# A state-space layer's input projection in one full-fp32 product instead of three split ones, with its parameter work in wider operations

## The chip, the core and the metric

One core of a Trainium2 chip runs the whole program. The metric is the device time of one execution in microseconds (us), median over several runs; less is better. The engines are TensorE (PE; its weight loads are a row of their own, PEld), VectorE (DVE), ScalarE (ACT), GpSimd (POOL) and SyncE (SP), which here only starts DMA transfers. Each engine works through its own instructions strictly in the order in which the program gives them; engines wait for each other by semaphores.

## What is computed

Two layers of a decoder trunk on 256 positions with 2048 channels, batch 1. Layer 0 mixes tokens with a state-space (S5) layer, layer 1 with a gated recurrence; each is followed by a SwiGLU. Scale, shift and gate of every norm come from a conditioning vector through the big matrix `w_ada`. The change touches the S5 layer:

```python
h = rmsnorm(x, norm_g[i, 0]) * (1.0 + sc1) + sh1
u = h @ w_in                                   # the input projection: 2048 x 2048
ug = u.reshape(bsz, seq, 128, 16)              # 128 groups of 16 channels
dt = exp(log_dt); mag = exp(lr * dt)
a = mag * (cos(li * dt) + i sin(li * dt))      # 64 complex states per group
b = (a - 1) / lambda * B                       # (128, 64, 16)
s_l = a * s_(l-1) + b u_l                      # a scan along the 256 positions
y = real(C s) + d_skip * u
y = gelu(y); val, gate = split(y @ w_glu); out = val * sigmoid(gate)
```

## The kernel before

The activations lie channels by positions: `X` is 128 partitions x 16 tiles x 256 positions. A matrix product takes 128 output channels at a time (a tile), as a sum over 16 (or 11, or 22) blocks of 128 input channels.

**Products in three parts.** TensorE takes a rounded fp32 format (`F32R`) in one pass. To stay accurate, each operand is split in a high part and a rest: ACT copies the weights to `wh` (L453), DVE computes `wl = raw - wh` (L468), and `H` holds high and low part of the activations. In the S5 projection, `into` (L874 and on) issues for each block `wh*h0`, `wh*h1` and `wl*h0` (L877 to L879). Elsewhere the first two are one product 512 columns wide.

**The weight stream.** Class `Stream` holds one list of items of 1 MB or less, in the order in which they are used: weights (`w`), and rows of `w_ada`. The latter are either `a` (a multiply-and-sum on DVE, L472), or `p` and `q` (four products on PE side by side in four column strips, L480; every fourth item ends with an ACT eviction to `par`, L486, and later with `rows_out`, L495 to L501, which turns the row into columns). Loads go out on SP's queue into four buffers `raw` (`NRAW = 4`); `step` first asks for the load of the item four places ahead, which waits until that buffer is free. `used` and `ahead` split the next weights, and do the `a` and `p` items, whenever a half block of weights (a slot) has been used up.

**The S5 layer** (`s5_layer`) has a prologue and a loop of 16 rounds, one for each tile. The prologue runs the first 31 or so items, in which shift and scale of the first norm are computed, beside `prep` (tables of the powers of `a`, on DVE), the sums of squares (ACT squares, POOL adds them up, `sq_add`) and the first parameters. Then `norm` writes `H`.

In round `t` PE runs the 16 blocks of tile `t` of the projection, and between them, by the table `fill`, pieces of other tiles:
- `states(t-1)`: 8 products `pv` (L346) of the tile's input `U` with `G`, then a `chain` on DVE: turn the phases back, scan, turn forward (L356 to L367);
- `outs(t-2)`: 12 products into `py` (L385, L387), then 16 ACT gelus (L915), each on 32 partitions and 64 columns;
- `gen2(t+1)`: transposes of `gs` into `pg` (`tr`, L306), each half evicted by ACT into `G` (L307), and between them `tt`, products into `pt` (L314), which DVE completes (L316); in the next round ACT copies `pt` in 16 pieces into `T` (L320, called `late`). `pg` and `pt` have one buffer each.

After the blocks: `u2(t)`, 16 ACT copies of the tile into `U` (L329); `gen_p(t+1)`, the phase table of a tile, six DVE operations (L285 to L287) and an ACT copy into `d0` (L289); `gen_gl(t+2)`, which builds the tile's `gs` and `ls` from its B and C: 4 ACT copies (L258) and 16 POOL operations (L251, L267); `load_bc(t+3)`, a DMA on ACT's queue (L94).

Of the kernel before, what the change touches and what calls it, by code (L numbers as in the profile page):

```python
# [75 lines left out]
class S5:  # L76
# [3 lines left out]
    def __init__(self, nc, const, gen, ps, lam, bcd, ident):  # L80
        self.nc, self.const, self.gen, self.ps = nc, const, gen, ps
        self.lam, self.bcd, self.ident = lam, bcd, ident
        self.work = None
        self.gt = {}
        self.bct = {}

    def load(self):
        self.lam_t = self.const.tile([P, 4, 64], F32, name="s5lam")
        self.nc.sync.dma_start(self.lam_t, self.lam)

    def load_bc(self, t):
        if t < 16:
            bct = self.gen.tile([P, 4, 4, 16], F32, tag="bct", bufs=2, name=f"bct{t}")
            (self.nc.scalar if self.work else self.nc.sync).dma_start(bct, self.bcd[t])  # L94
            self.bct[t] = bct

    def prep(self, w):
# [9 lines left out]
        self.ph = c.tile([P, 2, 2, N, 8], F32, name="s5ph")
        self.gs = c.tile([P, 2, 4, 4, 32], F32, name="s5gs")
        self.ls = [c.tile([P, 2, 4, 5, 32], F32, name=f"s5ls{i}") for i in range(4)]
        self.d0 = [c.tile([P, 4, 64], F32, name=f"s5d0{i}") for i in range(2)]  # L110
        self.T = [c.tile([P, 4, 4, 32], F32, name=f"s5T{i}") for i in range(3)]
        self.id4 = c.tile([P, 32], F32, name="s5id")
        nc.gpsimd.memset(self.gs, 0.0)
        for i in range(4):
            nc.gpsimd.memset(self.ls[i], 0.0)
        for i in range(2):
            nc.gpsimd.memset(self.d0[i], 0.0)
        for i in range(3):
            nc.gpsimd.memset(self.T[i], 0.0)
# [11 lines left out]
        def cmul(o, a, b):  # L131
# [15 lines left out]
            v.tensor_tensor(o[:, 0], m[:, 0], n[:, 1], SUB)  # L147
            v.tensor_tensor(o[:, 1], m[:, 1], n[:, 0], ADD)
# [49 lines left out]
        f = self.al[:, 0:2, :, 0]  # L198
# [38 lines left out]

    def gen_gl(self, t):

        if t >= 16:  # L240
            return
        nc, g = self.nc, self.gen
        e = nc.gpsimd
        bct = self.bct.pop(t)
        sl = slice(4 * t, 4 * t + 4)
        B = [bct[:, i] for i in range(2)]
        C = [bct[:, 2 + i] for i in range(2)]
        m = [g.tile([P, 4, 5, 16], F32, tag=f"gm{i}", bufs=1, name=f"gm{i}_{t}") for i in range(2)]

        def prod(out, a, pw, n):  # L250
            e.tensor_tensor(out[:, :, 0:n], bc(a, 2, n), bc(pw, 3, 16), MUL)  # L251

        agr, agi = self.ag[:, 0, sl], self.ag[:, 1, sl]
        alr, ali, aln = (self.al[:, i, sl] for i in range(3))
        for ri in range(2):
            for h in range(2):
                pp = slice(64 * h, 64 * h + 64)
                nc.scalar.activation(self.gs[pp, ri, :, 3, 16 * h:16 * h + 16], B[ri][pp], AF.Copy)  # L258
        for (x, pr, pi, dst, n, op1, pi2, op2) in (
                (C, alr, ali, self.ls[t % 4], 5, SUB, aln, SUB),  # L260
                (B, agr[:, :, 0:3], agi[:, :, 0:3], self.gs, 3, SUB, agi[:, :, 0:3], ADD)):
            for ri, (u, w_, op) in enumerate(((pr, pi, op1), (pi2, pr, op2))):
                prod(m[0], x[0], u, n)
                prod(m[1], x[1], w_, n)
                for h in range(2):
                    pp = slice(64 * h, 64 * h + 64)
                    e.tensor_tensor(dst[pp, ri, :, 0:n, 16 * h:16 * h + 16], m[0][pp, :, 0:n], m[1][pp, :, 0:n], op)  # L267

    def gen_p(self, t):
# [3 lines left out]
        nc, g = self.nc, self.gen  # L273
        sl = slice(4 * t, 4 * t + 4)
        pt = g.tile([P, 2, 4, 8, 8], F32, tag="pt", bufs=3, name=f"pt{t}")
        lo = [bc(self.ph[:, i, 0, sl], 2, 8) for i in range(2)]
        hi = [bc(self.ph[:, i, 1, sl], 3, 8) for i in range(2)]
        e = nc.vector if self.work else nc.gpsimd
        for i in range(2):
            if self.work:  # L280
                pm = self.work.tile([P, 2, 4, 8, 8], F32, tag="sm", bufs=1, name=f"pm{i}_{t}")
            else:
                pm = g.tile([P, 2, 4, 128], F32, tag="G", bufs=2, name=f"pm{i}_{t}")
                pm = pm[:, :, :, 0:64].rearrange("p i r (a b) -> p i r a b", a=8)
            e.tensor_tensor(pm[:, 0], lo[0], hi[i], MUL)  # L285
            e.tensor_tensor(pm[:, 1], lo[1], hi[1 - i], MUL)
            e.tensor_tensor(pt[:, i], pm[:, 0], pm[:, 1], ADD if i else SUB)  # L287
        d0 = self.d0[t % 2]
        nc.scalar.activation(d0[:, :, 1:64], bc(self.dec[:, sl], 2, 63), AF.Copy)  # L289
        self.gt.setdefault(t, {}).update(pt=pt, d0=d0)  # L290

    def gen2(self, t):
# [3 lines left out]
        nc, g = self.nc, self.gen  # L296
        gs, ls = self.gs, self.ls[t % 4]
        d = self.gt.setdefault(t, {})
        d["T"] = T4 = self.T[t % 3]

        def tr(i):
            if i == 0:
                d["G"] = g.tile([P, 2, 4, 128], F32, tag="G", bufs=2, name=f"G{t}")
            pg = self.ps.tile([P, 4, 128], F32, tag="pg", bufs=1, name=f"pg{t}_{i}")
            for r in range(4):
                nc.tensor.transpose(pg[:, r], gs[:, i, r], self.ident)  # L306
            nc.scalar.activation(d["G"][:, i], pg, AF.Copy)  # L307

        def tt():

            d["tp"] = pt = self.ps.tile([P, 4, 32], F32, tag="pt", bufs=1, name=f"pt{t}")
            for i in range(2):
                for r in range(4):
                    nc.tensor.matmul(pt[32 * r:32 * r + 32], gs[:, i, r, 3], ls[:, i, r, 0:4], start=(i == 0),  # L314
# [3 lines left out]
        def ev(q):  # L318
            for r in range(4):
                nc.scalar.activation(T4[32 * q:32 * q + 32, r, q:4], d["tp"][32 * r:32 * r + 32, 0:4 - q], AF.Copy)  # L320
        return [lambda: tr(0), tt, lambda: tr(1), lambda: [ev(q) for q in range(4)]]

    def u2(self, t, u):
# [1091 lines left out]
```

## Time and profile before

| | |
|---|---|
| median of 3 runs | 2536.26 us (2527.78 to 2536.91) |
| the profiled execution | 2531.59 us, its span 2529.4 us |
| mean granted clock of TensorE | 0.965 of full |
| PE, DVE, ACT, POOL busy | 2408.7, 1963.4, 1348.5, 386.4 us |
| prologue, to the first product of the projection | 0 to 97.5 us |
| `U` of tile 0, of tile 15 (ACT, L329) | from 114.10, from 393.93 us |

How to read it: PE is busy for 95% of the span, but records of products overlap and their ends are modelled, so that a stretch with PE "busy" need not be limited by PE. The first 430 us are the S5 layer and its output product; what follows runs on PE almost without gaps. A row of the timeline gives start, length, engine, line, operation, what it writes and reads, and in brackets the idle time before it and what ended it. The difference between the starts of two rows is what a step costs in the stream.

### The profile page before, as it was taken

How to read it: one execution, taken by the hardware profiler on the slowest of the kernel's cores; microseconds unless marked ns; L12 is line 12 of the kernel's file. 1: busy time of each engine (PE TensorE's matmuls, PEld its weight loads, DVE VectorE, ACT ScalarE, POOL GpSimd, SP SyncE). 2: the span in 40 equal slices, each digit the busy share in tenths (PEclk: the TensorE clock that was granted, in tenths of full speed). 3: DMA queues.
4: the chain of work that ended last, by engine and by line, in shares of the span. 5: the costliest groups of instructions: out<-in, count | busy, mean ns of one | idle time of the engine just before them, and what ended most of it. 6: DMA issues, size and time to landing. Idle time of an engine off the chain costs nothing. (4 is left out here: it accounts for less than half of the span.)

```text
span 2529.4 us, 37777 instructions
## 1 busy us (share of the span) xinstructions
PE 2408.7 (95%) x14456; PEld 2070.6 (82%) x14456; DVE 1963.4 (78%) x2743; ACT 1348.5 (53%) x2626; POOL 386.4 (15%) x418
## 2 busy tenths in 40 slices
PE   6888789999999999999999989999999999999998
PEld 1577678887888888888888878888788888888887
DVE  9689996888776787777889999888776555555565
ACT  1588776446444444444446775554644444444443
POOL 2879850001000000000003332010100000000000
PEclk7689888999999999999999999999999999999999
DMA  9845544987676798776886446879776456555453
GB/s 399 312 163 207 185 157 162 333 319 275 258 262 232 270 326 319 284 287 251 312 313 220 160 151 252 322 272 326 283 295 250 169 183 214 200 184 195 167 189 132
DMA packets 98277, 619.11 MB, mean 245 GB/s; under 512 B 11057, under 2 KB 15537, under 8 KB 38833
## 3 DMA queue, kind: packets, MB, share of 16 engines
q1 hardware_dynamic: 95936, 612.78, 67.1%
q10 hardware_dynamic: 2160, 3.93, 0.4%
q8 instruction: 113, 1.85, 0.3%
q14 instruction: 68, 0.55, 0.1%
HBM read 614.57 MB, written 2.10 MB: 244 GB/s over the span
## 5 line engine op out<-in xcount | busy, mean ns | idle before, releaser
L468 DVE TENSOR_TENSOR wl<-raw,wh 128x1024 fp32r<-128x1024 f32 (+1 forms) x856 | 934.8, 1113 | 370.6 <-ACT wh L453 367.3
L453 ACT ACTIVATE wh<-raw 128x1024 fp32r<-128x1024 f32 (+1 forms) x856 | 803.7, 956 | 677.7 <-PE d L576 204.8
L576 PE MATMUL d<-hid,wh 128*128 128x512 f32 x1344 | 464.9, 391 | 0.0
L576 PE MATMUL u<-H,wh 128*128 128x512 f32 x1290 | 447.6, 391 | 0.0
L576 PE MATMUL g<-H,wh 128*128 128x512 f32 x1290 | 447.6, 391 | 0.0
L575 PE MATMUL d<-hid,wl 128*128 128x256 f32 x1344 | 374.1, 278 | 0.0
L575 PE MATMUL u<-H,wl 128*128 128x256 f32 x1290 | 359.2, 278 | 0.0
L575 PE MATMUL g<-H,wl 128*128 128x256 f32 x1290 | 359.2, 278 | 0.0
L472 DVE CUSTOM_DVE_ANT_0 raw<-raw,cond 128x2048 f32<-128x2048 f32 x132 | 306.0, 2319 | 1.7 <-DMA raw<-in_wada 1.6
L576 PEld LDWEIGHTS d<-hid,wh 128*128 128x128 f32 x1344 | 252.3, 188 | 51.5
L576 PEld LDWEIGHTS u<-H,wh 128*128 128x128 f32 x1290 | 242.1, 188 | 48.7
L576 PEld LDWEIGHTS g<-H,wh 128*128 128x128 f32 x1290 | 242.1, 188 | 48.6
L575 PEld LDWEIGHTS d<-hid,wl 128*128 128x128 f32 x1344 | 252.4, 188 | 2.9
L575 PEld LDWEIGHTS u<-H,wl 128*128 128x128 f32 x1290 | 242.3, 188 | 3.9
L575 PEld LDWEIGHTS g<-H,wl 128*128 128x128 f32 x1290 | 242.3, 188 | 3.9
L764 ACT ACTIVATE gs<-gs 128x256 f32<-128x256 f32 x88 | 36.8, 418 | 202.4 <-DVE gs L613 202.4
L576 PE MATMUL lg<-H,wh 128*128 128x512 f32 x330 | 117.3, 398 | 0.0
L480 PE MATMUL pa<-raw,condz 128*32 128x512 f32 x480 | 90.7, 856 | 27.9 <-DMA raw<-in_wada 19.9
L662 POOL TENSOR_TENSOR rs_lru<-var_lru,mhalf 128x2 f32<-128x2 f32 x1 | 1.6, 1608 | 724.2 <-DVE var_lru L661 724.2
L662 POOL TENSOR_TENSOR rs_fin<-var_fin,mhalf 128x2 f32<-128x2 f32 x1 | 0.7, 695 | 723.8 <-DVE var_fin L661 723.8
L576 PE MATMUL xb<-H,wh 128*128 128x512 f32 x300 | 103.2, 389 | 0.0
L575 PE MATMUL lg<-H,wl 128*128 128x256 f32 x330 | 93.4, 283 | 0.0
(416 smaller groups left out, 4319.1 us busy)
## 6 DMA issues: line engine op xcount, KB each, us to landing
raw<-in_wada SPq DMA_DIRECT2D x192, 1024.0 KB, 5.7
raw<-in_gu SPq DMA_DIRECT2D x176, 1024.0 KB, 4.8
raw<-in_dn SPq DMA_DIRECT2D x128, 704.0 KB, 4.3
raw<-in_lruin SPq DMA_DIRECT2D x44, 1024.0 KB, 5.0
raw<-in_s5glu SPq DMA_DIRECT2D x32, 1024.0 KB, 5.6
raw<-in_lruout SPq DMA_DIRECT2D x32, 704.0 KB, 5.4
raw<-in_s5win SPq DMA_DIRECT2D x16, 1024.0 KB, 6.0
raw<-in_lruri SPq DMA_DIRECT2D x8, 512.0 KB, 5.5
```

Of the source, the lines that this page charges most:

```text
L453: nc.scalar.activation(dh, src, AF.Copy)
L468: self.nc.vector.tensor_tensor(*self.lazy.pop(0), SUB)
L472: self.nc.vector.tensor_tensor_reduce(t, t, self.cond, 1.0, 0.0, MUL, ADD, self.mod[:, n:n + 1])
L480: nc.tensor.matmul(self.bank[32 * c:32 * c + 32], self.condz[:, 4 * q + c], t[:, 512 * c:512 * c + 512], start=(q == 0), stop=(q == 3), ti ...
L575: mm(bank[:, 0], wl, x[:, 0], start=False, stop=False, skip_group_check=True)
L576: mm(bank, wh, x, start=False, stop=last, skip_group_check=True)
L662: nc.gpsimd.tensor_tensor(rs, var, self.mhalf, ALU.pow)
L764: nc.scalar.activation(g, g, AF.Silu)
```

## The change

The projection's weights are used as they were loaded, in fp32, with one product for each block; neither they nor the normed activations are split. In the code:

- `into` is one product of the loaded block with `hf`, the fp32 activations. `norm` writes `hf` alone, even tiles on ACT, odd ones on DVE.
- A new item kind `f` holds its `raw` buffer until the sixteenth block is through. While it is open, `load` asks for no more than three items behind it, and `ahead` does nothing (but in round 15, `ahead(True)`).
- The tables change their layout, so that real and imaginary part lie side by side: `gen_gl` has 8 POOL operations twice as wide, `gen_p` three DVE operations of 512 columns, and its copy into `d0` (`gen_d`) is twice as wide; the `chain` has one scan of 512 instead of two of 256.
- The parameters have more buffers. `gen_gl` runs four tiles ahead, `gen2` three, `gen_p` four; the last tiles use buffers of their own from lists, so that rounds 10, 13 and 15 have no `gen2`. Five `gen_p`, four `gen_gl` and three `gen2` move to the prologue.
- `fill` has a new order.
- The sums of squares are made on PE: each squared tile goes through two products with a column of ones.
- The buffers stand in the memory that `H` and the split weights take later: both are made at the start of round 15 (`late_tiles`).
- Of the 28 items of `w_ada` spread over the loop, 8 are `p` and 20 `a` (before 16 and 12), and the first 33 items come in a slightly different order.

```diff
 def into(bank, k):
-    wh, wl = st.next()
-    h = self.H[:, k]
-    nc.tensor.matmul(bank, wh, h[:, 0], start=(k == 0), stop=False)
-    nc.tensor.matmul(bank, wh, h[:, 1], start=False, stop=False)
-    nc.tensor.matmul(bank, wl, h[:, 0], start=False, stop=(k == 15))
+    nc.tensor.matmul(bank, st.next()[0], hf[:, k], start=(k == 0), stop=(k == 15))
...
 def load(self, upto):
+    if self.open is not None:
+        upto = min(upto, self.open + self.nraw)
...
+        if kind == "f":
+            self.pieces += [(t[:, k * P:k * P + P], None, k == n - 1, None) for k in range(n)]
+            self.open = i
+            self.done += 1
+            return
...
-    def ahead(self):
+    def ahead(self, past=False):
...
+            if self.open is not None and (not past or kind == "f" or self.done >= self.open + self.nraw):
+                return
             self.step()
...
     def gen_gl(self, t):
...
+        for x, pw, n, dst, op in ((2, al, 5, ls, SUB), (0, ag, 3, gs, ADD)):
+            m = [y[:, 0:128 * n].rearrange("p (r i c) -> p r i c", r=4, c=16) for y in mm]
+            for i in range(2):
+                a = 0 if i else n
+                e.tensor_tensor(m[i], bc(bct[:, x + i], 2, 2 * n), bc(pw[:, :, a:a + 2 * n], 3, 16), MUL)
+            m = [y[:, 0:128 * n].rearrange("p (a q c) -> p a q c", q=n, c=16) for y in mm]
+            for h in range(2):
+                pp = slice(64 * h, 64 * h + 64)
+                o = dst[pp, :, :, 0:n, 16 * h:16 * h + 16].rearrange("p r i q c -> p (r i) q c")
+                e.tensor_tensor(o, m[0][pp], m[1][pp], op)
...
     def gen_p(self, t):
...
+        v.tensor_tensor(pt, bc(self.lo[:, sl, 0], 2, 16), bc(hi[:, :, 8:24], 3, 8), MUL)
+        v.tensor_tensor(pm, bc(self.lo[:, sl, 1], 2, 16), bc(hi[:, :, 0:16], 3, 8), MUL)
+        pt, pm = self.pt[t].rearrange("p r i n -> p (r i n)"), pm.rearrange("p r a b -> p (r a b)")
+        v.tensor_tensor(pt, pt, pm, ADD)
...
 for t in range(16):
-    o, a, g = s5.outs(t - 2, gelu), s5.states(t - 1), s5.gen2(t + 1) if t else g
-    fill = {0: late, 3: a[0:2], 4: a[2:4], 5: a[4:], 6: o[0:1], 7: o[1:2], 8: o[2:3], 9: o[3:4],
-            10: o[4:], 11: g[0:1], 12: g[1:2], 13: g[2:3]}
+    n = t + 3 if t < 10 else {11: 13, 12: 14, 14: 15}.get(t, 16)
+    o, a, g = s5.outs(t - 2, gelu), s5.states(t - 1), s5.gen2(n)
+    fill = {0: late, 6: a[0:2], 7: a[2:5], 8: g[0:1], 9: g[1:2], 10: g[2:3], 11: o[0:1], 12: o[1:2],
+            13: o[2:3], 14: o[3:4], 15: o[4:]}
...
-    s5.gen_p(t + 1)
-    s5.gen_gl(t + 2)
-    s5.load_bc(t + 3)
+    s5.gen_d(t + 1)
+    if 0 < t < 11 or t == 14:
+        s5.gen_p(t + 4 if t < 11 else 15)
+    s5.load_bc(t + 5)
+    if t != 9:
+        s5.gen_gl(t + 4 if t < 9 else t + 3)
...
+def square(k):
+    sq = self.sqp.tile([P, T], F32, tag="sq", bufs=2, name=f"sq{k}")
+    nc.scalar.activation(sq, self.X[:, k], AF.Square)
+    for h in range(2):
+        nc.tensor.matmul(sums[:, 0, h:h + 1], sq[:, h * P:h * P + P], self.ones, start=(k == 0 and h == 0),
+                         stop=(k == 15 and h == 1), skip_group_check=True)
...
+items = [x for i in range(0, 12, 4) for x in ada(i, i + 4) + ada(i + 16, i + 20)]
+items += ada(12, 16) + ada(28, 29) + win[0:1] + ada(29, 32)
+items += win[1:3] + mix(win[3:], ada(32, 60), 9, 4)
...
-KINDS = "p" * 32 + "ppppaaaappppaaaappppaaaapppp" + "a" * 20 + "qqqp" + "a" * 56 + "qqqp" + "a" * 32 + "qqqp" + "a" * 12
+KINDS = "p" * 32 + "p" * 8 + "a" * 40 + "qqqp" + "a" * 56 + "qqqp" + "a" * 32 + "qqqp" + "a" * 12
```

More of the change, by code (lines that the diff above doesn't have):

```diff
@@ L102, in prep @@
         lr, li, ldt = (self.lam_t[:, i] for i in range(3))
-        self.dsk = self.lam_t[:, 3]
-        self.ag = c.tile([P, 2, N, 4], F32, name="s5ag")
-        self.al = c.tile([P, 3, N, 5], F32, name="s5al")
+        ag = self.far.tile([P, N, 3, 3], F32, name="s5ag")
+        al = self.far.tile([P, N, 3, 5], F32, name="s5al")
         self.dec = c.tile([P, N], F32, name="s5dec")
[L107 to L111, printed above, removed]
-        self.id4 = c.tile([P, 32], F32, name="s5id")
[L113 to L119, printed above, removed]
+        lo = self.far.tile([P, N, 2, 8], F32, name="s5lo")
+        hi = self.far.tile([P, N, 3, 8], F32, name="s5hi")
+        self.ag, self.al, self.lo, self.hi = ag, al, lo, hi
+        self.id4 = c.tile([P, 32], F32, name="s5id")
+        for x in self.gs + self.ls0 + self.d0 + self.T0:
+            nc.gpsimd.memset(x, 0.0)
         for q in range(4):
@@ L197, in prep @@
         v.tensor_tensor(u1, u1, u2, ADD)
[L198 removed]
+        f = two("f")
         v.tensor_tensor(f[:, 0], u1, den, MUL)
@@ L241, in gen_gl @@
             return
-        nc, g = self.nc, self.gen
+        nc = self.nc
         e = nc.gpsimd
-        bct = self.bct.pop(t)
+        bct, gs, ls = self.bct[t % 4], self.gs[t % 2], self.ls[t]
         sl = slice(4 * t, 4 * t + 4)
[L246 to L251, printed above, removed]
@@ L398, with __init__ @@
 class Stream:
-    def __init__(self, nc, raw, spl, items, nraw, npiece, cond, condz, ones, raw_mod):
-        self.nc, self.raw, self.spl = nc, raw, spl
+    def __init__(self, nc, raw, items, nraw, npiece, cond, condz, ones, raw_mod):
+        self.nc, self.raw, self.spl = nc, raw, None
         self.items, self.nraw, self.npiece = items, nraw, npiece
@@ L750, in ffn @@
             first = self.modulate(ps, f"f{layer}")
-            hp.tile([P, 48 if layer else 32], F32, name="gap")
+            hp.tile([P, 72 if layer else 56], F32, name="gap")
             hid = hp.tile([P, 22, 2, T], F32R, name=f"hid{layer}")
@@ L891, in s5_layer @@
             norm(8, 12)
+            for k in range(8):
+                into(bank, k)
             st.step()
[L893 removed]
+            for k in range(8, 12):
                 into(bank, k)
[L895 to L912 removed]
+            st.rows_out()
+            ready(12, 16)
+            norm(12, 16)
             def gelu(t, r, q, py):
@@ L942, in s5_layer @@
                         upto(k - 3)
+                    if t == 15 and k == 4:
+                        st.ahead(True)
                     for f in fill.get(k, ()):
@@ L1155, in g4 @@
                     self.split(dst[j], xb[:, j])
-            big.tile([P, 16], F32, name="gap")
+            big.tile([P, 40], F32, name="gap")
             ext = big.tile([P, 6, 2, T], F32R, name="yext")
@@ L1215, in lru_layer, with late_tiles @@
             self.sq_add(15)
+    def late_tiles(self):
+        late = self.ctx.enter_context(self.tc.tile_pool(name="late", bufs=1, side="right", reuse_waits="tile"))
+        self.H = late.tile([P, 16, 2, T], F32R, name="H")
+        self.st.spl = weight_slots(late)
     def run(self):
@@ L1280, in run @@
         items += dn[1][0] + gu[1][1] + dn[1][1]
-        assert sorted(x[2] for x in items if x[0] not in "wr") == list(range(192))
-        spl = weight_slots(split)
-        self.st = Stream(nc, raw, spl, items, NRAW, NPIECE, cond, condz, self.ones, self.modr)
+        assert sorted(x[2] for x in items if x[0] not in "wrf") == list(range(192))
+        self.st = Stream(nc, raw, items, NRAW, NPIECE, cond, condz, self.ones, self.modr)
         self.cond = cond
```

281 lines of the change are left out of this document (128 added, 153 removed).

## The prediction

> **What bounds the kernel now.** The change ends with the S5 layer, so I read first the busy times by stretch: prologue, and nine whole rounds of the loop.
>
> ```profile
> core 0: us, PE busy (x) PEld busy (x) DVE busy (x) ACT busy (x) POOL busy (x), PEclk, DMA share, GB/s
> 0.00:97.40 97.40, 67.90 (x340) 21.48 (x340) 72.99 (x224) 24.57 (x68) 48.63 (x72) 0.69 0.96 383
> 180.40:348.00 167.60, 135.31 (x1122) 113.84 (x1122) 164.63 (x191) 137.38 (x516) 143.98 (x147) 0.94 0.54 192
> ```
>
> The prologue is bound by its loads (DMA share 0.96). The loop at first sight is bound by DVE: 164.6 of 167.6 us, 18.3 us of a mean round of 18.6. That invites the conclusion that whatever DVE loses is won. So I read next ACT's timeline for one undisturbed round, gelu to gelu.
>
> ```profile
> 180.42 3.62 ACT L915 ACTIVATE X<-py 32x64 f32<-32x64 f32 x16
> 184.06 0.60 ACT L307 ACTIVATE G<-pg 128x512 f32<-128x512 f32 x1
> 185.47 0.60 ACT L307 ACTIVATE G<-pg 128x512 f32<-128x512 f32 x1 [0.81 <-PE pg L306]
> 186.07 1.06 ACT L453 ACTIVATE wh<-raw 128x1024 fp32r<-128x1024 f32 x1
> 187.03 3.64 ACT L329 ACTIVATE U<-in 32x64 f32<-32x64 f32 x16
> 190.69 0.41 ACT L289 ACTIVATE s5d<-s5dec 128x252 f32<-128x252 f32 x1
> 190.76 0.33 ACTq L94 DMA_DIRECT2D bct<-in_s5bc  x1
> 191.01 1.07 ACT L258 ACTIVATE s5gs<-bct 64x64 f32<-64x64 f32 x4
> 192.11 3.83 ACT L320 ACTIVATE s5T<-pt 32x128 f32<-32x128 f32 x16
> 195.97 1.06 ACT L453 ACTIVATE wh<-raw 128x1024 fp32r<-128x1024 f32 x1
> 197.30 0.44 ACT L915 ACTIVATE X<-py 32x64 f32<-32x64 f32 x2 [0.27 <-PE py L387]
> ```
>
> It took 16.9 us, and ACT hardly paused: 0.81 us for the transposes, 0.27 for the outputs. So behind DVE stands a second loop, nearly as long, in which ACT and PE hand work to each other. Relieving DVE doesn't shorten it; the new order of the program may lengthen it. I therefore price the new round along this loop. The whole stage is measured between these two rows:
>
> ```profile
> 114.10 3.64 ACT L329 ACTIVATE U<-in 32x64 f32<-32x64 f32 x16
> ```
>
> ```profile
> 393.93 3.66 ACT L329 ACTIVATE U<-in 32x64 f32<-32x64 f32 x16
> ```
>
> From `U` of tile 0 to `U` of tile 15 are 279.8 us for 15 rounds.
>
> **Prices on PE.** No product of the new kind is in the trace, so it is bounded by its neighbours.
>
> ```profile
> 101.92 1.07 PE L480 MATMUL pa<-raw,condz 128*32 128x512 f32 x8
> 102.92 0.38 PE L877 MATMUL in<-H,wh 128*128 128x256 f32 x1
> ```
>
> ```profile
> 103.61 0.28 PE L879 MATMUL in<-H,wl 128*128 128x256 f32 x1
> 103.73 0.60 PE L306 MATMUL pg<-ident,s5gs 128*128 128x128 f32 x4
> 104.17 0.95 PE L501 MATMUL pc<-ones,par 128*128 128x1 f32 x8
> 104.98 0.36 PE L877 MATMUL in<-H,wh 128*128 128x256 f32 x1
> ```
>
> ```profile
> 124.87 0.64 PE L314 MATMUL pt<-s5ls,s5gs 128*32 128x128 f32 x16 [0.15 <-ACT s5T L320]
> ```
>
> ```profile
> 195.03 0.37 PE L877 MATMUL in<-H,wh 128*128 128x256 f32 x1
> ...
> 196.05 0.36 PE L877 MATMUL in<-H,wh 128*128 128x256 f32 x1
> ```
>
> A split product takes 0.12 us (103.61 to 103.73), a block's three 0.36. An fp32 product stands as two records. An item's four fp32 products of 512 columns run side by side in four strips: 1.00 us (101.92 to 102.92). One with 256 columns has half of that, at most 0.50. The four products with one column (x8) show what a record costs that has next to nothing to stream: 0.81/8 = 0.10 us of weight load. If the loads run under the record before, 0.45 us a block, which I take; if not, 0.45 + 0.20 = 0.65; from below, were each record one 256-column pass of 0.12, 0.24. So a tile takes 7.2 us of PE instead of 5.8: PE gets dearer by 1.4 us a round, and only ACT and DVE are relieved.
>
> [...]
>
> Other pieces: four transposes 0.44 (103.73 to 104.17); `tt` 0.6; a piece of `outs` 1.02 - 0.36 = 0.66 (195.03 to 196.05 is one block and one piece); two of `pv` are four records, at 0.10 each 0.4.
>
> **DVE and POOL, round by round.**
>
> ```profile
> L468 DVE TENSOR_TENSOR wl<-raw,wh 128x1024 fp32r<-128x1024 f32 x18 | 26.5, 1474 | 0.0
> L472 DVE CUSTOM_DVE_ANT_0 raw<-raw,cond 128x2048 f32<-128x2048 f32 x10 | 26.1, 2613 | 0.0
> ```
>
> ```profile
> L286 DVE TENSOR_TENSOR pm<-s5ph 128x256 f32<-128x256 f32 x18 | 16.9, 940 | 0.0
> L285 DVE TENSOR_TENSOR pm<-s5ph 128x256 f32<-128x256 f32 x18 | 14.8, 825 | 0.3
> L287 DVE TENSOR_TENSOR pt<-pm 128x256 f32<-128x256 f32 x18 | 14.7, 819 | 0.6
> L365 DVE TENSOR_TENSOR S<-sn,pt 128x512 f32<-128x512 f32 x9 | 10.2, 1130 | 0.0
> ```
>
> These rows are of the same nine rounds. The splits go: 26.5/9 = 2.9 us a round. `gen_p` cost 46.4/9 = 5.2 and becomes three operations of 512 columns, 3 x 1.13 = 3.4 (five of them in the prologue, where DVE has room). The `a` items rise from 26.1/9 = 2.9 to 2.25 x 2.61 = 5.9 in rounds 7 to 14. That leaves DVE 18.3 - 2.9 - 5.2 + 3.4 + 3.0 = 16.6 us at most, less in the others: off the path if the loop of ACT and PE is longer. The chain keeps its work (one wide scan for two). POOL was busy 144/9 = 16 us a round; the same elements in half the operations are no more, but it may write the next tile's `ls` only when the outputs six tiles back are read, just before a round begins, with two thirds of its 16 us still to do: it holds the first transposes until 10.7 at most. What follows them waits until 12.8 anyway, as shown now; without that cover it would cost 1 us a round.
>
> **The new round.** Zero is the first gelu. ACT's order is now gelus, `U`, `gen_d`, `gs`, `T`, first `G`. From the rows: 3.64, 3.66, 0.51 (0.32, and 0.19 for twice the columns, as 0.60 of `G` against 0.41), 1.10 and 3.86: `T` ends at 12.8. PE meanwhile runs block 15, blocks 0 to 6 (to 3.5), waits for `U` (8 of 16 copies at 5.5, all at 7.3), does `pv`, blocks 7 to 9 and the first transposes by 10.5, and then waits: `tt` needs `pt`, which `T`'s copies free at 12.8. In program order everything behind `tt` waits with it: block 10, second transposes, `outs`, and so the next gelus. The rest is 0.1 + 0.6 + 0.45 + 0.44 + 4 x (0.45 + 0.66) + 0.14 = 6.2. A full round takes 12.8 + 6.2 = 19.0, where the undisturbed one took 16.9. Without `gen2` PE sets the end: `U` at 7.4, then 1.2 `pv`, blocks 7 to 10 1.8, `outs` 4.4, 0.1: 15.0; with `gen2` but no `T` before it 16.5.
>
> **Loads.** A weight tile now keeps its buffer for a whole round. Where three items stand between two weights, the next weight's load can't start before the tile is done, and SP's later loads queue behind it: at the ends of rounds 0, 6, 10 and 14.
>
> ```profile
> DMA to landing us min/median/max: 4.9/6.0/12.0
> ```
>
> That is 5 us of PE standing. In round 7 it ends before `U` and `T` do and costs nothing; if that cover were gone, 5 us. In round 11 no `T` covers it: 5.3 + 7 x 0.45 + 1.6 + 1.8 + 1.5 + 4.6 = 18.0. In round 1 it makes 17.0 (5.3, blocks 3.2, a half-speed window 1.7, `pv` 1.6, blocks and transposes 1.6, `tt` and the rest 3.6). Two rounds have an ACT eviction of a `p` row ahead of their gelus, which waits for two `p` items on PE: 3.0 each (2 x 1.00, block 15, 0.6 eviction).
>
> **The sum.** One row more, the table load ahead of the first gelu:
>
> ```profile
> 139.35 1.28 ACT L915 ACT_TABLE_LOAD   x1
> ```
>
> Round 1 17.0; round 2, from `U`, 9.1 + 6.2 + 1.3 for that load = 16.6; rounds 3 to 9 7 x 19.0 + 6.0 = 139.0; 10, 13: 15.0 each; 11: 18.0; 12: 19.0; 14: 16.5; 15: 18.0, on ACT (gelus, `U`, `gen_d`, `T` 11.7, four splits of the next weights 3.9, seven copies to `H` at about 0.35, an estimate from `G`'s 0.60 for twice the columns).
>
> Together 274.1 against 279.8: -5.7. Tile 0 needs no low parts. Before, `rows_out` ended at 104.98 and `U` started 9.1 later. After, twelve blocks ahead cost 1.1 more, then shift, scale and first norm take about 1.2 (estimate), four blocks 1.8, transposes and `tt` 1.1: `U` at about 110, -4. The rest of the prologue I cost at nothing, as loads cover it: on PE 64 records for the squares, 6.5 us or double at half clock, beside 67.9 busy of 97.4; on POOL more memsets but no adds of squares; 2 more parameter loads on SP's queue, 0.25 MB, 0.6 us. The three `gen2` now in it stand where no row eviction queues right behind `T`; without that some 4 us each. Later stages: `H` and weight slots only move; 0.
>
> Last, the clock.
>
> ```profile
> 234.00:238.00 4.00, 0.80 (x7) 0.83 (x8) 3.86 (x5) 3.05 (x13) 3.79 (x5) 1.00 0.49 205
> 238.00:241.40 3.40, 3.40 (x17) 1.51 (x15) 3.33 (x4) 3.05 (x10) 3.18 (x5) 0.50 0.00 0
> 311.70:314.20 2.50, 0.34 (x3) 0.13 (x2) 2.47 (x3) 2.28 (x9) 2.36 (x4) 1.00 0.51 216
> 314.20:317.60 3.40, 3.37 (x27) 2.42 (x28) 3.23 (x6) 2.63 (x8) 3.19 (x5) 1.00 0.04 5
> ```
>
> A gap of 3.2 us on PE was followed by 3.4 us at half clock, one of 2.2 us was not. The new round has two gaps of 2 to 2.4 us, the second right before PE sets the end. A window at half clock there costs 1.7 us; I charge it in a quarter of the eight full rounds, 3.4.
>
> [...]
>
> So -5.7 - 4 + 3.4 = -6 on the profiled execution's 2531.6 us. The median is 2536.3; from there 2530.
>
> **Rivals.**
> *DVE's relief counts in full.* If PE and ACT overlap better than I read, the round falls to what DVE keeps, 16.6: 15 x 16.6 = 249 instead of 279.8, with tile 0 -35: 2501. For it: DVE at 98%. Against: ACT's row of a round without a pause.
> *The product isn't what it says.* At 0.24 a block, nine rounds lose 5 x 0.21 and the four without `T` 8 x 0.21 of PE's tail, -16: -22, 2514. Against: 1.00 us for an item's four products.
> *Slower: the clock.* If the gap before `tt` does drop the clock in every full round, with its tail of 6 us in two windows, 9 x 2.5 us, and the shorter rounds 4 x 1.7: +29 on -10 is +19, 2555. It decides from a gap of somewhere between 2.2 and 3.2 us.
> *Slower: loads not hidden.* 0.65 a block: nine rounds x 1.0, four x 1.6, +3 in the others: +18 on -6, 2548.
>
> **Chances.** This kernel's measurement can tell about 0.5% (12.7 us) from no change. Forecast 0.45, of which 0.06 beyond -12.7 and 0.39 within; DVE 0.17, product 0.12, clock 0.19 (0.03 within), loads 0.07 (half). So faster 0.35, same 0.45, slower 0.20. Range 2502 to 2554: it takes in both ends of the block's price and nearly the two outer rivals; the forecast's own is 2520 to 2540.
>
> **What would show it.** One product a block at 0.45 us; DVE idle for some us in each round; full rounds of 19 us with ACT's `T` and `tt` back to back, PE waiting there for ACT; rounds 10 and 13 at 15; `U` of tile 0 near 110 and of tile 15 near 384. Rounds of 17 or less, DVE still at 98%, or granted clock below 0.85 in the loop prove me wrong.

## The result and the profile after

| | before | after |
|---|---|---|
| median | 2535.68 us (4 runs, 2527.78 to 2536.91) | 2561.49 us (4 runs, 2560.09 to 2561.91) |
| ratio | | 1.0116, 95% interval 1.0097 to 1.0134 |
| the profiled execution: span | 2529.4 us | 2558.3 us |
| `U` of tile 0 starts | 114.10 | 131.56 |
| `U` of tile 15 starts | 393.93 | 418.63 |
| from there to the end of the span | 2135.5 | 2139.7 |
| DVE, POOL busy | 1963.4, 386.4 us | 1910.6, 309.7 us |

The change made the kernel 1.2% slower, where the forecast was -6 us. The span grew by 28.9 us: 17.5 in the prologue (forecast -4), 7.2 in the loop (forecast -5.7, and 3.4 more charged for the clock), 4.2 behind the loop (forecast 0). The two rows that bound the loop, in ACT's timeline:

```profile
131.56 3.18 ACT L338 ACTIVATE U<-in 32x64 f32<-32x64 f32 x14
...
418.63 3.66 ACT L338 ACTIVATE U<-in 32x64 f32<-32x64 f32 x16 [1.91 <-PE in L907]
```

**The loop** is, in its full rounds, the one that was forecast. ACT's timeline from the gelus of round 2 to those of round 3, and PE's for the place where it waits:

```profile
165.85 3.62 ACT L930 ACTIVATE X<-py 32x64 f32<-32x64 f32 x16
169.48 2.97 ACT L338 ACTIVATE U<-in 32x64 f32<-32x64 f32 x13
172.46 0.68 ACT L338 ACTIVATE U<-in 32x64 f32<-32x64 f32 x3
173.16 0.62 ACT L301 ACTIVATE s5d<-s5dec 128x504 f32<-128x504 f32 x1
173.69 0.81 ACT L271 ACTIVATE s5gs<-s5bc 64x64 f32<-64x64 f32 x4
174.52 3.83 ACT L329 ACTIVATE s5T<-pt 32x128 f32<-32x128 f32 x16
178.37 0.60 ACT L315 ACTIVATE s5G<-pg 128x512 f32<-128x512 f32 x1
180.15 0.60 ACT L315 ACTIVATE s5G<-pg 128x512 f32<-128x512 f32 x1 [1.18 <-PE pg L314]
184.50 1.56 ACT L930 ACTIVATE X<-py 32x64 f32<-32x64 f32 x7 [3.75 <-PE py L394]
```

```profile
178.40 0.64 PE L323 MATMUL pt<-s5ls,s5gs 128*32 128x128 f32 x16
```

`T` ends 12.5 us after the first gelu, `tt` starts at that moment, and the next gelus come 6.1 later: a round of 18.65 us where 12.8 + 6.2 = 19.0 was forecast. Busy times over the loop, of the changed kernel and of the one before:

```profile
131.56:418.63 287.07, 238.46 (x1415) 196.11 (x1414) 186.74 (x219) 185.95 (x760) 127.35 (x88) 0.88 0.42 164
```

```profile
114.10:393.93 279.83, 233.11 (x1788) 201.34 (x1789) 258.49 (x321) 227.09 (x846) 211.08 (x217) 0.88 0.48 172
```

In order stand length, PE, PEld, DVE, ACT, POOL, the granted clock, the DMA share and GB/s. DVE lost 72 us of 258, ACT 41, POOL 84, and the loop became longer all the same. The mean granted clock is 0.88 in both; where in the loop it falls is another matter, to which the part on the prediction returns.

**The prologue** is another one than the forecast's. The same columns for three stretches of it, before and after:

```profile
35.00:60.00 25.00, 19.45 (x100) 6.45 (x96) 23.64 (x63) 7.80 (x24) 11.05 (x14) 0.69 1.01 421
60.00:80.00 20.00, 18.45 (x84) 6.31 (x84) 10.89 (x38) 2.14 (x6) 13.23 (x22) 0.51 0.99 368
80.00:97.40 17.40, 12.73 (x84) 5.11 (x80) 6.67 (x12) 11.34 (x32) 16.43 (x22) 0.70 0.90 353
```

```profile
35.00:60.00 25.00, 23.41 (x104) 13.31 (x96) 23.36 (x85) 3.90 (x11) 0.00 (x0) 0.50 0.81 307
60.00:80.00 20.00, 17.64 (x94) 8.76 (x93) 5.04 (x16) 5.08 (x18) 8.35 (x8) 0.62 0.72 261
80.00:97.40 17.40, 12.65 (x100) 5.70 (x96) 14.39 (x16) 7.39 (x26) 16.75 (x13) 0.75 0.99 375
```

The loads no longer bind it: their share falls from 1.0 to 0.81 and 0.72. Between 35 and 60 PE has work for 23.4 of 25 us, at half clock. PE's timeline there shows why (`pa` is a parameter item, `nrm_s` the squares, two tiles in each row):

```profile
44.44 1.93 PE L496 MATMUL pa<-raw,condz 128*32 128x512 f32 x8
46.30 1.87 PE L859 MATMUL nrm_s<-ones,sq 128*128 128x1 f32 x8
48.10 1.93 PE L496 MATMUL pa<-raw,condz 128*32 128x512 f32 x8
51.05 1.86 PE L859 MATMUL nrm_s<-ones,sq 128*128 128x1 f32 x8 [1.02 <-ACT sq L857]
52.85 1.93 PE L496 MATMUL pa<-raw,condz 128*32 128x512 f32 x8
```

Items 8 to 15 now start 4.5 us apart (34.68 to 66.26 for seven), and a load of 1 MB takes 2.5 at 421 GB/s. So the last squares end at 71, and `rs` (the factor of the norm) comes at 71.4 instead of 65.8. POOL begins its four `gen_gl` behind `rs`, and PE waits for them at the transposes (first row: POOL of the kernel before; second: POOL now; the others: PE now):

```profile
65.83 0.71 POOL L662 TENSOR_TENSOR rs_s<-var_s,mhalf 128x2 f32<-128x2 f32 x1 [5.83 <-DVE var_s L661]
...
71.36 0.70 POOL L688 TENSOR_TENSOR rs_s<-var_s,mhalf 128x2 f32<-128x2 f32 x1 [57.47 <-DVE var_s L687]
...
81.66 0.81 PE L314 MATMUL pg<-ident,s5gs 128*128 128x128 f32 x4 [1.49 <-POOL s5gs L281]
...
93.14 1.12 PE L314 MATMUL pg<-ident,s5gs 128*128 128x128 f32 x4 [1.62 <-POOL s5gs L281]
...
105.71 1.12 PE L314 MATMUL pg<-ident,s5gs 128*128 128x128 f32 x4 [2.17 <-POOL s5gs L281]
```

### The profile page after: what moved, and what is told of

It reads as the page before. It is cut to its first block, busy times and chain, and to the rows that moved or that the text cites. A ratio compares the mean times of both kernels' runs of the same rounds, so it can differ in the third digit from the quotient of the medians.

```text
span 2558.3 us, 36848 instructions
## 1 busy us (share of the span) xinstructions
PE 2430.0 (95%) x14176; PEld 2081.0 (81%) x14176; DVE 1910.6 (75%) x2653; ACT 1310.0 (51%) x2584; POOL 309.7 (12%) x268
## 5 line engine op out<-in xcount | busy, mean ns | idle before, releaser
L484 DVE TENSOR_TENSOR wl<-raw,wh 128x1024 fp32r<-128x1024 f32 (+2 forms) x824 | 887.1, 1099 | 353.0 <-ACT wh L469 349.9
L469 ACT ACTIVATE wh<-raw 128x1024 fp32r<-128x1024 f32 (+2 forms) x824 | 769.1, 952 | 673.7 <-PE d L597 199.7
L488 DVE CUSTOM_DVE_ANT_0 raw<-raw,cond 128x2048 f32<-128x2048 f32 x140 | 327.7, 2346 | 0.1
L907 PE MATMUL in<-s5h,raw 128*128 128x256 f32 x512 | 160.5, 439 | 17.9 <-DMA raw<-in_s5win 13.0
L907 PEld LDWEIGHTS in<-s5h,raw 128*128 128x128 f32 x512 | 99.1, 217 | 35.7 <-issue 11.1
L496 PE MATMUL pa<-raw,condz 128*32 128x512 f32 x416 | 71.2, 782 | 23.0 <-DMA raw<-in_wada 19.7
```

The lines of the kernel that those rows point to most:

```text
L469: nc.scalar.activation(dh, src, AF.Copy)
L484: self.nc.vector.tensor_tensor(*self.lazy.pop(0), SUB)
L488: self.nc.vector.tensor_tensor_reduce(t, t, self.cond, 1.0, 0.0, MUL, ADD, self.mod[:, n:n + 1])
L496: nc.tensor.matmul(self.bank[32 * c:32 * c + 32], self.condz[:, 4 * q + c], t[:, 512 * c:512 * c + 512], start=(q == 0), stop=(q == 3), ti ...
L907: nc.tensor.matmul(bank, st.next()[0], hf[:, k], start=(k == 0), stop=(k == 15))
```

## The experiments

The first theory from this: the squares on PE, and behind them POOL's `gen_gl`, make the prologue late; the place of `outs` behind `T` makes the loop long. The rivals: the fp32 product is too dear, buffers held by it keep the loads back, or the clock. Single runs of the kernel before spread from 2526 to 2537 us, so a kernel that ran once is read by its stages. How steady a stage is, three runs with the same prologue show: the change, and twice the one with `outs` first, start `U` of tile 0 at 131.56, 131.88 and 131.96.

**The prologue, first attempts.**

```diff
 if i >= 8:
-    square(2 * i - 16)
-    square(2 * i - 15)
+    self.sq_add(2 * i - 16, nc.gpsimd)
+    self.sq_add(2 * i - 15, nc.gpsimd)
```

> The squares of the first norm are summed by POOL again, as before the change; PE keeps none of them until the two sums at the end. If PE at half clock, with the one-column records of the squares between its parameter products, bounds the prologue: the parameter items 8 to 15 come 2.6 us apart instead of 4.5, rs is out near 62 instead of 71, and everything behind it moves up by as much: U of tile 0 at about 122 instead of 131.6, the whole run about 9 us shorter (2551). If the prologue is late because raw buffers are held by the new product or by the three gen2 alone: U of tile 0 stays within 2 us of 131.6.

Measured: `U` of tile 0 at 132.8, 2568.6 us. The theory failed here: `rs` didn't come earlier (72.0). PE was through with the sums at 58.5, but `var` stood on DVE behind the rest of `prep`, and POOL's sums slowed `prep`. Two equal operations of this run on DVE, the first while POOL was adding, the second after:

```profile
51.85 0.92 DVE L169 TENSOR_TENSOR prm<-p 128x128 f32<-128x128 f32 x1
...
63.38 0.38 DVE L169 TENSOR_TENSOR prm<-p 128x128 f32<-128x128 f32 x1
```

`prep` ended at 71.8 instead of 61.6, and PE, which now has the broadcast of `rs` at item 17 of its queue and not at 21, stood there:

```profile
72.78 1.22 PE L692 MATMUL nrb_s<-ident,rs_s 128*128 128x128 f32 x4 [8.88 <-POOL rs_s L688]
```

The next two start POOL's `gen_gl` early; the second has the edit above as well:

```diff
+if i in (8, 9):
+    s5.gen_gl(i - 8)
...
-s5.gen_gl(0)
-s5.gen_gl(1)
```

> gen_gl(0) and gen_gl(1) are given to POOL in the middle of prep, before the statistics of the norm instead of after them; the squares stay on PE. If the chain of gen_gl on POOL, which starts at 72 and gates the three gen2 in PE's queue, holds the prologue: the waits of the transposes for POOL (1.5, 1.6 and 2.2 us on PE) go, gen2(2) starts near 95 instead of 105.7, U of tile 0 at about 123, the run about 8 us shorter. If PE alone (the squares at half clock) is the bound: U of tile 0 within 2 us of 131.6, the waits move to the loads.

> Squares on POOL and gen_gl(0), gen_gl(1) early, both. If the two together are what made the prologue late, the loads bound it again (DMA share above 0.95 until 100) and U of tile 0 comes at about 113, as in the kernel before (114.1) or at the 110 of the forecast; the run is 18 us shorter than the changed kernel (2542). If something else holds it (the fp32 product, the buffers): U of tile 0 stays above 120.

Measured: `U` of tile 0 at 135.8 (2565.1 us) and 138.2 (2572.7 us); both miss. The waits for POOL at the first transposes did go, but two `gen_gl` beside `prep` held DVE longer still, so that `rs` came at 79.9 and 81.7; in the second, ACT's squares waited for POOL's sums behind `gen_gl`, and PE for ACT. The row is from the timeline of the run with both:

```profile
58.29 3.24 PE L496 MATMUL pa<-raw,condz 128*32 128x512 f32 x16 [13.04 <-ACT par L502]
```

So the theory of one cause fell. Work moved onto POOL there is paid for by DVE; and the order in which waits stand in PE's queue had to be tested by itself.

**One part of the change alone, in the kernel before.**

```diff
 if i >= 10:
-    self.sq_add(2 * i - 20, nc.gpsimd)
-    self.sq_add(2 * i - 19, nc.gpsimd)
+    square(2 * i - 20)
+    square(2 * i - 19)
```

> The kernel before with one part of the change alone: the squares of the first norm are summed by PE, two per item in items 10 to 17, instead of by POOL; nothing else. If the squares make PE the bound of the prologue here too: items 10 to 17 come 4.5 us apart instead of 2.6, U of tile 0 moves from 114.1 to about 122, and the run takes 8 us more (2545). If PE has room for them, as the forecast said: U of tile 0 at 114 or earlier, since POOL no longer slows the prep on DVE, and the run is within 3 us of the kernel before.

Measured: `U` of tile 0 at 126.08, 12.0 later than before, and 2547.75 us beside 2526.52 of the kernel before on the same chip. Two stretches of it look like the changed kernel's (clock 0.50, DMA share 0.73 and 0.67):

```profile
45.00:60.00 15.00, 13.35 (x62) 8.15 (x59) 12.30 (x43) 3.66 (x10) 0.00 (x0) 0.50 0.73 259
60.00:80.00 20.00, 17.92 (x79) 9.66 (x79) 0.16 (x1) 4.57 (x14) 3.65 (x5) 0.50 0.67 222
```

The squares on PE cost this kernel 12 us of prologue on their own, where 8 were expected. Its loop took 6.3 us more as well (286.2); I have no run that says why.

**The order of the prologue's waits**, with the squares on POOL and on PE:

```diff
-    if i == 17:
+    if i == 21:
         next(stat, None)
-    if 18 <= i < 22:
-        for k in range(4 * i - 72, 4 * i - 68):
+        for k in range(16):
             nc.vector.tensor_tensor(self.X[:, k], self.X[:, k], self.rs, MUL)
...
-    if i in (20, 24):
-        for f in s5.gen2(i // 4 - 5):
-            f()
-        s5.gen_gl(i // 4 - 3)
+    if i == 25:
+        for f in s5.gen2(0):
+            f()
+        s5.gen_gl(2)
 st.late = True
-for f in s5.gen2(2):
+for f in s5.gen2(1):
     f()
+s5.gen_gl(3)
...
 norm(12, 16)
+for f in s5.gen2(2):
+    f()
```

> Two things together: the squares of the first norm on POOL again, and the order of the prologue's steps as in the kernel before: rs is broadcast at item 21 instead of 17, gen2(0) stands at item 25, gen2(1) behind the last item, gen2(2) right ahead of tile 0's last four blocks, so that PE's queue stands at fewer places for POOL. With the squares on POOL alone, rs came no earlier (72.0), since POOL's sums slowed the prep on DVE, and PE stood 8.9 us at the broadcast for it, with the loads. If the place of the waits in PE's queue is what holds the loads: the DMA share stays above 0.9 until 97, U of tile 0 comes at about 117 instead of 131.6, and the run takes 2546. If what holds the prologue is POOL's chain of gen_gl whatever the order (four times 10 to 12 us from rs on): U of tile 0 stays above 127.

> The order of the prologue's steps as in the run with both (rs broadcast at item 21, gen2(0) at 25, gen2(1) behind the items, gen2(2) ahead of the last four blocks), but the squares stay on PE as in the change. If the squares on PE cost the prologue time of their own (items 8 to 15 at 4.5 us each until 71, DMA share 0.5 to 0.8 from 45 to 75): U of tile 0 lies some 8 us behind that of the run with both, at about 125, and 6 us ahead of the change. If only the order counts: both runs have the same U of tile 0. If only the squares count: this run is at 131.6 as the change.

Measured: 128.85 (2562.9 us) with the squares on POOL, 142.66 (2572.6 us) with them on PE, which none of the expectations had. With the squares on POOL the DMA share now stayed at 0.93 and more until 80; with them on PE it was 0.62 from 45 to 60 and 0.72 from 60 to 80. In both, the second `gen2` had a new wait. The timeline of the run with the squares on POOL:

```profile
93.52 1.65 DVE L295 TENSOR_TENSOR s5pt<-s5pt,pm 128x512 f32<-128x512 f32 x1
95.09 0.24 DVE L325 SCALAR_TENSOR_TENSOR pt<-s5id,s5dsk,pt 128x32 f32<-128x32 f32 x1
...
95.37 3.81 ACT L329 ACTIVATE s5T<-pt 32x128 f32<-32x128 f32 x16 [7.36 <-DVE pt L325]
...
99.23 1.08 PE L323 MATMUL pt<-s5ls,s5gs 128*32 128x128 f32 x16 [7.27 <-ACT s5T L329]
```

To be read from below: PE waits 7.3 us for ACT's copies into `T`, these 7.4 for the last DVE operation of the first `tt`, and that stands on DVE behind four `gen_p`, of which nearly every operation takes 1.2 to 2.0 us beside POOL, and 0.69 in the loop with POOL idle. In the run with the squares on PE the same wait for `T` took 12.9 us. So 128.85 fits the branch "above 127" of the expectation, but not for its reason. The forecast had put the `gen_p` there because "DVE has room".

**gen_p out of the prologue**, which completes the eight combinations:

```diff
-    if 22 <= i < 27:
-        s5.gen_p(i - 22)
...
-    if 0 < t < 11 or t == 14:
-        s5.gen_p(t + 4 if t < 11 else 15)
+    for n in {0: (0, 1, 2), 1: (3, 5), 2: (4, 6)}.get(t, (t + 4,) if t < 11 else (15,) if t == 14 else ()):
+        s5.gen_p(n)
```

> The changed kernel with gen_p(0) to gen_p(4) moved out of the prologue into rounds 0 to 2; squares on PE and the order of the prologue as in the change. If gen_p beside gen_gl (each slows the other, 9.6 us a gen_gl alone and 11.4 to 12.5 beside it) is a part of the 17.5 us: the last of the three gen2 starts near 101 instead of 105.7 and U of tile 0 comes at about 127. If the squares alone make the prologue late: U of tile 0 within 2 us of 131.6.

> gen_p out of the prologue and the squares on POOL, the order as in the change (rs broadcast at item 17, gen2 at items 20 and 24 and behind 27). If the place of the waits in PE's queue is a cause of its own: PE still stands about 9 us at the broadcast for rs and again at the transposes for POOL, and U of tile 0 stays at about 126, ten behind the 115.6 of the run that has the order too. If squares and gen_p are the whole cause: 116.

> gen_p out of the prologue and the order of the kernel before, the squares on PE as in the change. It differs in the prologue by the squares alone from the run whose tile 0 started at 115.6. If the squares on PE cost what they cost in the kernel before (12.0 us): U of tile 0 at about 127. If their time is hidden once the rest is in order: within 2 us of 115.6.

The eighth has all three edits, and `outs` first (below), which doesn't touch the prologue:

> The changed kernel with outs and gelus first in the round, the squares on POOL, the order of the prologue as in the kernel before, and gen_p(0) to gen_p(4) moved out of the prologue into rounds 0 to 2 (in the run without this, four of them stood on DVE ahead of the scalar_tensor_tensor of gen2(1), and PE waited 7.3 us for T). If those waits are what still held tile 0: U of tile 0 at 121 instead of 128.9, the loop at 266, so 7 us faster than the kernel before. If POOL's gen_gl chain from rs on (68 plus four times 10 to 12) holds it: U of tile 0 above 126, and the run level with the kernel before.

| squares | order of the waits | gen_p | `U` of tile 0 |
|---|---|---|---|
| PE | the change's | prologue | 131.6 (the change) |
| POOL | the change's | prologue | 132.8 |
| PE | before's | prologue | 142.7 |
| PE | the change's | rounds 0 to 2 | 127.6 |
| POOL | before's | prologue | 128.9 |
| POOL | the change's | rounds 0 to 2 | 127.0 |
| PE | before's | rounds 0 to 2 | 131.6 |
| POOL | before's | rounds 0 to 2 | 115.6 |

Of the three runs of this step, the first two came as expected (127 and 126); in the second, PE stood 12.0 us at the broadcast of `rs`. The third missed: 131.6 instead of 127. The forecast of 121 for the last row was too careful; the price of `gen_p` was not 7 but 13 us.

With all three back, 16.0 of the 17.5 us are back. From that corner each edit undone alone costs much: squares on PE 16.0, the change's order 11.4, `gen_p` in the prologue 13.3. From the change each one mended alone gives 4.0 at most, and two of them make it worse. So the edits don't add up; what each is worth depends on the others:

- In the change's order the squares make 1.2 us of difference at most. `rs` comes at 71.4 to 72.1 in all four of these runs, and with the squares on POOL, PE stands in its queue for it (8.9 and 12.0 us). In before's order the squares on PE cost 13.8 and 16.0.
- `gen_p` in the prologue costs 4.0 and 5.8 us in the change's order and 11.1 and 13.3 in before's, in which the second `gen2` waits behind it.
- Before's order gains 3.9 and 11.4 us with the squares on POOL, and loses 11.1 and 4.0 with them on PE. It is several moves at once (the broadcast of `rs`, the scaling of `X`, three `gen2` and two `gen_gl`), which no run separates.

Taking one wait away can show the next. The rows of the version with all three, in ACT's timeline:

```profile
115.58 3.18 ACT L338 ACTIVATE U<-in 32x64 f32<-32x64 f32 x14
...
387.51 3.66 ACT L338 ACTIVATE U<-in 32x64 f32<-32x64 f32 x16 [1.55 <-PE in L897]
```

This version has a median of 2525.48 us (10 runs), beside 2533.03 of the kernel before on the same chip (20 runs): ratio 0.9974, interval 0.9959 to 0.9988. It beats both kernels, by little. Of the 16.0 us only 11.0 reach the median, beside `outs` first alone (2536.5, below): the loop takes 271.9 us, 5 to 6 more than there. The `gen_p` moved into its first rounds is one candidate, but the rounds that are longer are 5, 7 and 13, and no run says why.

One more try put `var` ahead of the last level of `prep` on DVE:

```diff
-    for _ in range(2):
+    for _ in range(2 if i < 7 else 0):
         next(prep, None)
...
-    for _ in prep:
-        pass
 stat = self.norm_stat(mm, "s5")
 next(stat)
 next(stat)
+for _ in prep:
+    pass
```

> The same, and var of the first norm put ahead of the last level of prep in DVE's queue, so that rs doesn't wait for it. If rs is the start of the chain that sets tile 0 (rs, gen_gl(0) to gen_gl(3) on POOL, three gen2 on PE): rs at 60 instead of 68 to 72, U of tile 0 some 8 us ahead of the run with the late var, at about 113, and 15 us faster than the kernel before. If the chain of gen_gl isn't the bound: U of tile 0 within 2 us of that run.

Measured: `U` of tile 0 at 135.1, 2543.29 us, ratio 1.0047 (1.0031 to 1.0064). A miss: `rs` came at 58.4, but what was left of `prep` now ran beside POOL's `gen_gl` until 97, and the short operation that completes `tt` stood behind it. From the waits of that run, 60 to 131 us (total, times, longest):

```profile
PE pt L323 <- ACT s5T L329: 18.5, 1, 18.5
ACT s5T L329 <- DVE pt L325: 16.9, 1, 16.9
```

**The loop.** Only the table of pieces is changed:

```diff
-fill = {0: late, 6: a[0:2], 7: a[2:5], 8: g[0:1], 9: g[1:2], 10: g[2:3], 11: o[0:1], 12: o[1:2],
-        13: o[2:3], 14: o[3:4], 15: o[4:]}
+fill = {0: late + o[0:1], 1: o[1:2], 2: o[2:3], 3: o[3:4], 4: o[4:], 6: a[0:2], 7: a[2:5],
+        8: g[0:1], 9: g[1:2], 10: g[2:3]}
```

> Only the order within a round: the pieces of outs stand at blocks 0 to 3 and the gelus behind block 4, ahead of pv and gen2; before they stood at blocks 11 to 15, behind the transposes that wait for T. If the chain of ACT and PE (gelus, U, T, then tt, transposes, outs, gelus) sets the round of 19 us, it is now broken up: full rounds fall to about 17, what DVE keeps (16.6), and U of tile 0 to U of tile 15 take about 260 us instead of 287, the run 25 us less (2536). If the price of the fp32 product on PE, its waits for weights, or the clock set the round: the loop stays within 5 us of 287. U of tile 0 unchanged at 131.6.

> The changed kernel with outs and gelus ahead of pv and gen2 in each round, nothing else, now timed. Its loop took 265.9 us instead of 287.1; with U of tile 0 still at 131.9 it should stand level with the kernel before, within 0.3%, and 1.0% ahead of the change.

Measured: 265.9 us from `U` to `U` instead of 287.1 (266.7 in the timed run), with `U` of tile 0 unmoved:

```profile
131.88 3.19 ACT L338 ACTIVATE U<-in 32x64 f32<-32x64 f32 x14
...
244.77 3.83 ACT L329 ACTIVATE s5T<-pt 32x128 f32<-32x128 f32 x16
248.63 3.62 ACT L930 ACTIVATE X<-py 32x64 f32<-32x64 f32 x16
252.90 0.60 ACT L315 ACTIVATE s5G<-pg 128x512 f32<-128x512 f32 x1 [0.66 <-PE pg L314]
...
397.77 3.66 ACT L338 ACTIVATE U<-in 32x64 f32<-32x64 f32 x16 [0.81 <-PE in L907]
```

In the round shown the gelus follow `T` directly, and the transposes come when `T` has long freed `pt`: the chain is cut. Of the 26 us by which the change lost, this gives 25 back, though not all where they were lost: the prologue is as late as in the change, and the loop is now 13.9 us shorter than in the kernel before. The median is 2536.5 (10 runs), the ratio to the kernel before 1.0018 (1.0004 to 1.0031). The 4.2 us behind the loop are gone too (2135.4 in the timed run). The rival of the buffers: PE waits 13.0 us in the change's loop for the projection's weights (three times, none in the kernel before), about what the forecast had charged, and still 13.3 here. So these waits are a price of the change, but not what this edit took away.

**The price of the product.** In one run half of the products are left out; in another (second edit) all stay, and blocks 3 to 9 are multiplied once more, into a place that nobody reads:

```diff
+w = st.next()[0]
+if k % 2 == 0:
+    nc.tensor.matmul(bank, w, hf[:, k], start=(k == 0), stop=(k == 14))
...
+if more and 3 <= k < 10:
+    nc.tensor.matmul(more, w, hf[:, k], start=False, stop=(k == 9), skip_group_check=True)
```

> The changed kernel with every second product of the input projection left out (the sum runs over half of the blocks, so the output is another one); loads, order and everything else stay. PE loses 8 x 0.45 = 3.6 us a tile. If the price of the fp32 product on PE made the loop longer than before, the rounds fall by all of 3.6: U of tile 0 to U of tile 15 at about 233 instead of 287. If the chain of ACT and PE sets the round, only the three products left out behind the wait for T count, 1.4 a full round, and some more in the rounds without gen2: about 265.

> The changed kernel with blocks 3 to 9 of each tile from 1 to 15 multiplied twice, the second time into a part of the bank that nobody reads: 7 x 0.45 = 3.1 us more of PE a round, in the stretch where PE waits for U and T. With half of the products left out the granted clock in the loop fell from 0.88 to 0.70 and the loop became longer. If the clock follows how much PE streams: granted clock above 0.93 in the loop, half-clock windows gone from most rounds, and U of tile 0 to U of tile 15 no longer than 287, rather 280. If PE's work as such sets the round: about 40 us longer.

Neither theory of the first expectation held: with half the products the loop took 301.3 us, 14.3 more. With 105 products more it took 289.8, 2.7 more, although they are 47 us of PE at 0.45 each; that is nearer to the second expectation's first branch (no longer than 287) than to its other (40 longer). The busy times of the two loops (columns as above):

```profile
125.65:426.99 301.34, 232.68 (x1177) 188.19 (x1175) 175.14 (x216) 185.42 (x760) 125.39 (x93) 0.70 0.41 153
```

```profile
130.33:420.13 289.80, 260.87 (x1625) 220.89 (x1624) 179.12 (x222) 185.95 (x760) 124.42 (x89) 0.95 0.43 165
```

The granted clock is 0.70 with half of the products, 0.88 with all, and 0.95 with the 105 more. So the product's price doesn't set the round in the stretch that was doubled, where PE waits for `U` and `T`. PE's own work there is nearly free, and less of it goes with a lower clock. More work behind `T`, in blocks 10 to 15, was not tried.

## Why the prediction was wrong

- **The failed step** is "The rest of the prologue I cost at nothing, as loads cover it". It weighed "64 records for the squares, 6.5 us or double at half clock" against "67.9 busy of 97.4", the mean of the prologue. The rows took 14.9 us, 1.87 per item, between 35 and 80 us, where PE had already been busy 19.5 + 18.5 of 45 us at a granted clock of 0.69 and 0.51, and where each item had 2.5 us. An item's own work on PE was 1.87 for its products and a quarter of 1.87 for `rows_out`, so 2.3; with the squares it was 4.2. The prologue came 21.5 us later than forecast (17.5 instead of -4). Where the loads cover, they cover only as long as PE needs no more for an item than the load does.
- **Three gen2 in the prologue** were costed by whether a row eviction queues behind `T`. What held them was ahead of them: POOL's `gen_gl`, which starts only behind `rs`, and, in before's order, `gen_p` on DVE ("where DVE has room") ahead of the operation that completes `tt`. The step looked at the room of an engine and not at who stands behind in its queue. From the good end of the table, the order and `gen_p` each undone alone cost 11.4 and 13.3 us. (In program order, the kernel before already had two `gen2`, two `gen_gl` and one `gen_p`, the last on POOL, ahead of `U` of tile 0; the change has two `gen2`, two `gen_gl` and four `gen_p` more there.)
- **The fp32 block**: 0.45 forecast, the author's estimate between the 0.24 and the 0.50 that the neighbours' rows gave. Right: at full clock four blocks take 1.78 us from start to start (412.24 to 414.02), 0.445 each. A block is two records, where each of its three split products was one, of 0.12 us.

```profile
412.24 1.95 PE L907 MATMUL in<-s5h,raw 128*128 128x256 f32 x8
414.02 0.33 PE L392 MATMUL py<-U,s5T 128*128 128x64 f32 x2
```

- **The full round**: 19.0 and the two evictions give 139.0 for rounds 3 to 9; measured from the gelus at 165.85 to those at 306.15, 140.3. Right, and the experiment with `outs` first shows that it was this chain: from `U` to `U` the same seven rounds take 127.0 there instead of 140.4. Rounds 1 and 2 took 34.3 where 33.6 was forecast.
- **Rounds 10 to 15** were undersized: 101.5 forecast, 112.5 measured (306.15 to 418.63); that is 11.0 of the 13.0 us by which the loop missed its sum of 274.1. Where PE doesn't wait for `T`, PE sets the end, and half-clock windows count in full. Rounds 10, 11, 13, 14 and 15 had one or two of them each (3.4 us long) and took 1.5 to 3.1 us more than forecast. I had charged the clock to full rounds, where ACT's `T` hides most of it: the round shown above took 18.65 at a mean granted clock of 0.82. Round 15 was forecast on ACT, but PE set it (the wait at 418.63). Round 13, from the gelus at 361.51 to those at 379.62, took 18.1 instead of 15.0, and 16.1 in the run with more products:

```profile
361.90:365.30 3.40, 3.08 (x15) 2.37 (x13) 3.40 (x3) 3.22 (x16) 3.34 (x2) 1.00 0.57 212
365.30:368.70 3.40, 1.30 (x6) 0.89 (x6) 0.50 (x2) 3.19 (x16) 3.32 (x3) 1.00 0.98 414
368.70:372.10 3.40, 3.25 (x13) 3.07 (x14) 0.00 (x0) 3.25 (x14) 2.19 (x3) 0.51 0.71 292
372.10:375.50 3.40, 3.40 (x9) 2.68 (x10) 3.28 (x5) 1.82 (x9) 0.00 (x0) 0.50 0.04 14
```

- **DVE off the path**: right, as PE never waits for DVE in the change's loop. Its busy time was 186.7/15 = 12.4 us in the mean round, but the bound of 16.6 didn't hold for every round: rounds 8, 9 and 11 had 16.6, 17.4 and 19.8. With `outs` first DVE is on the path, and PE waits 9.9 us for its `S`.
- **Behind the loop**, put at nothing, 4.2 us were lost. They went with `outs` first; no run says more of them.
- **The rivals**: the slower one by the clock gave 2555, near the result, but by luck. (Its -10 is -5.7 - 4, the forecast without the 3.4 charged for the clock.) Its main part, 2.5 us in each full round, didn't happen (rounds 3 to 9: 139.0 forecast, 140.3 measured); its small part, in the shorter rounds, did; and for the prologue it kept the forecast's -4. The loads not hidden under the product (0.65 a block) didn't come; nor did DVE's relief in full: even with `outs` first the loop took 265.9 us and not 249.

## What to carry to other kernels

Price work that moves into a stretch bound by loads against the time of one load, at the clock granted there, not against the stretch's mean. Before a producer is put into another stage, list what stands behind it on its engine: here an operation of 0.24 us behind `gen_p` held PE for 7 us. Several waits can lie behind each other, so that mending each alone shows nothing or a loss; try them together, and then undo one at a time from the good end.

## What the runs showed of the hardware

- **The clock fell after windows with little work on PE, not only after a gap.** In the rows of round 13 PE was busy 1.30 of 3.40 us, 38%, with no gap longer than 1.10 us, and the next two windows were granted half clock (0.51 and 0.50). In the loop of this trace the clock changes on a grid of 3.41 us. There, each of the 11 windows at full clock in which PE was busy for 1.6 us or less was followed by half clock; of the eleven with 1.7 to 2.4 us three were (2.29 us from 348.23 on, but not the 1.97 just before); of those with more, none. The forecast had put the limit between gaps of 2.2 and 3.2 us (the second is 3.49 us long in PE's row at 237.21 of the kernel before). The two runs with fewer and more products (0.70, 0.95) say the same over a whole loop. Busy time alone isn't the measure, though: between 35 and 60 us of the prologue, with one-column products between parameter products, PE was busy 23.4 of 25 us at a granted clock of 0.50.
- **DVE and POOL slowed each other.** An operation of `prep` on two inputs took 0.38 us alone and 0.92 beside POOL; `gen_p`'s 0.69 became 1.2 to 2.0, and a `gen_gl` on POOL took 9.6 us ahead of `gen_p` (72.0 to 81.6) and up to 12.5 beside it (93.2 to 105.7); with `gen_p` out of the prologue and the squares on POOL, the two between the transposes at 82.38 and at 101.69 took 19.3 together, 9.65 each. The rows show how much each slowed the other, not why. With the squares on POOL alone, this put the end of `prep` at 71.8 instead of 61.6, so that `rs` was no earlier than in the change.
